# A fourth seven-product chunk in the late projection pairs, with two of the four weight sums of each group on GpSimd

## The chip, the cores and the metric

The kernel runs on one NeuronCore of a Trainium2 chip. The metric is the device time of one execution in microseconds (us); 2 us are about 0.2% of it. The engines are named as the profile names them: PE is the matrix engine, PEld its weight loads, DVE the vector engine, ACT the scalar engine, POOL is GpSimd, and SP issues most DMAs. Each engine works through its own instructions in a fixed order, and waits on semaphores for what others must deliver first.

## What is computed

One residual layer over 256 tokens of width 2048, in float32, followed by an RMSNorm. The layer projects the normalised input `h` to many column blocks, runs two token mixers, and merges their results:

```python
h = _rms_norm(x, norm_g)
proj = jnp.einsum('bsd,dn->bsn', h, w_in)          # q k v o za gates xb zb ga gb
ya = _mlstm_branch(q, k, v, o, za, gates, ...)     # 256 x 2048
yb = _rglru_branch(xb, zb, ...)                    # 256 x 2048
ya = jnp.einsum('bsw,wd->bsd', ya, w_branch_a)
yb = jnp.einsum('bsw,wd->bsd', yb, w_branch_b)
merged = sigmoid(ga) * ya + sigmoid(gb) * yb
out = _rms_norm(x + jnp.einsum('bsd,de->bse', merged, w_out), final_g)
```

The change touches the last projections: `w_branch_b`, the `gb` and `ga` blocks of `w_in`, `w_branch_a` and `w_out`. Each is a product of a 256 x 2048 activation with a 2048 x 2048 weight.

## The kernel before

**Numbers in two parts.** A float32 value is split into a rounded part `hi` (ACT copies it to the matmul type) and a rest `lo` (DVE subtracts `hi` from the value), and a product is made of three matmuls, hi·hi, hi·lo and lo·hi. So each weight chunk that arrives by DMA as `raw` (128 x 1024 float32, 512 KB) costs an ACT copy to `whi` and a DVE subtraction to `wlo` before PE can use it. There are six `raw` buffers and four each of `whi` and `wlo`.

**Pairs.** From line 163 on, `pair` computes two 512-column blocks at once. The inner dimension of 2048 is cut into eight chunks, `kq` = 0 to 7, of 256 rows each. A *plain* chunk (line 229) loads one `raw` for each of the two blocks and multiplies 2 blocks x 2 row halves x 2 token halves = 8 products of three matmuls each: 24 matmuls of 512 columns.

A chunk whose number is in `kqs` goes through `products` (line 186): the 2 x 2 blocks of weights and the 2 x 2 blocks of activations are combined by the Strassen-Winograd scheme, with seven products in place of eight, so 21 matmuls in place of 24. It needs sums of weight blocks, made as the weights arrive: `t1` (the tile tagged `vhi`) by the subtractions on lines 199 and 200, `t2` (`vlo`) by lines 203 and 204, each of the four on 128 x 512 elements. Line 203 reads the half of `t1` that line 200 made. Then `t1`, `t2` and the second `raw` are split into `whi` and `wlo` (lines 180 and 181: three tiles of 1024 columns) and half of the first `raw` into `b11` (512 columns). The same two `raw` tiles, 1 MB, are loaded as for a plain chunk. There is one `t1` and one `t2`, so the next group's `t1` is written only when the last reader of this one is done.

Four of the seven products gather in PSUM tiles `aux`, the others in `acc`. After the last such chunk of the pair, lines 252 to 256 combine the `aux` tiles into the destination (one ACT copy, four DVE additions that read PSUM), and line 262 adds `acc`.

The activations need sums too, once for each chunk number and activation: `make_form` (line 271) builds them with one addition, four sums on 128 x 128 and a split of 512 columns, all on DVE but one ACT copy.

**Which chunks.** The tables at the top say it. `S_WB`, `S_GB`, `S_GA` and `S_WA` list the chunk numbers of the two pairs of `w_branch_b`, `gb`, `ga` and `w_branch_a`: 0, 2 and 4 in each of these eight *late pairs*. `L_WB` to `L_WA` are the places in the order of the eight chunks at which they stand. The pair of `w_out` (`S_WO`, line 1034) has four such chunks already, as places 0, 2, 4 and 6. The order in time is: `w_branch_b` (two pairs), `gb` (two), `ga` (two), `w_branch_a` (two), one block of `w_out` without products (line 1021), the `w_out` pair, the last `w_out` block. Earlier pairs (`S_V`, `S_OZ`) are not touched.

**Order.** A scheduler orders each engine's instructions when the program is built. Weight loads, splits and sums are marked urgent (`urgent()`), so they stand in weight order, ahead of other work; the forms fill in between. After that the order of each engine is fixed.

POOL does little before: masks at the start, and small tensors of one column for the normalisation of the four heads (lines 860 and 861).

Of the kernel before, what the change touches and what calls it, by code (L numbers as in the profile page):

```python
# [10 lines left out]
F32R = mybir.dt.float32r  # L11
# [8 lines left out]
NB = 512  # L20
# [3 lines left out]
EPS = 1e-6  # L24
NEG = -1e30

S_WB, S_GB, S_GA, S_WA = [((0, 2, 4), (0, 2, 4))] * 4
S_OZ = (((4, 0), (2, 4)), ((4,), (1,)), ((4, 0), (2, 5)), ((4, 0), (0, 2)))
S_V = (((4,), (4,)), ((4,), (4,)))
S_WO = (0, 1, 2, 4)  # L30
L_WB, L_GB, L_GA, L_WA = ((0, 2, 4), (0, 2, 4)), ((0, 2, 4), (0, 2, 4)), ((0, 2, 4), (0, 2, 4)), ((0, 2, 4), (1, 3, 5))
L_WO = (0, 2, 4, 6)
H_FORMS = (4, 0)
PLAN = (dict(Y=('c0', '', '', 'c1',),
# [17 lines left out]
def hybrid_encoder(ctx: ExitStack, tc: tile.TileContext, x, xt, pk, bif, fg, wg, wi, wr, wa, wb, wo, out):  # L52
# [107 lines left out]
    def four(v):  # L160
        return v.rearrange("p (a b) -> p a b", b=S)

    def pair(src, xhi, xlo, forms, kqs, dst, b11, epilogue, sums=None, places=None, calm=False):
        aps = []
        accs = [acc_pair()[1] for _ in range(2)]
        banks = [[v[:, :NB], v[:, NB:]] for v in accs]
        began = set()
        places = places or kqs
        rest = [kq for kq in range(KT // KC) if kq not in kqs]
        seq = [kqs[places.index(i)] if i in places else rest.pop(0) for i in range(KT // KC)]  # L170
        kl = seq[-1]

        def mm(ps, a, b, wh, wl, stop):
            pe.matmul(ps, a, wh, start=id(ps) not in began, stop=False)  # L174
            began.add(id(ps))
            pe.matmul(ps, a, wl, start=False, stop=False)  # L176
            pe.matmul(ps, b, wh, start=False, stop=stop)  # L177

        def split(hi, lo, v):
            act.copy(hi, v)  # L180
            dve.tensor_sub(lo, v, f(hi))  # L181

        def wpair():
            return [wp.tile([P, KC * NB], F32R, tag=t, name=name(t), bufs=4) for t in ("whi", "wlo")]

        def products(kq, last):
            lf, rt_ = slice(0, NB), slice(NB, 2 * NB)
            with urgent():
                r1, r2 = [wp.tile([P, KC * NB], F32, tag="raw", name=name("raw"), bufs=6) for _ in range(2)]
                sp.dma_start(r1, src[0][kq])  # L190
                sp.dma_start(r2, src[1][kq])
                bh, bl = b11()
                split(bh, bl, r1[:, lf])
                if sums:
                    t1, t2 = sums()
                else:
                    t1, t2 = [four(hp.tile([P, 2 * NB], F32, tag=t, name=name("t"))) for t in ("vhi", "vlo")]
                v1, v2 = four(r1), four(r2)
                dve.tensor_sub(t1[:, :2], v1[:, 2:], v1[:, :2])
                dve.tensor_sub(t1[:, 2:], v2[:, :2], v1[:, 2:])  # L200
                h1, l1 = wpair()
                split(four(h1), four(l1), t1)
                dve.tensor_add(t2[:, :2], t1[:, 2:], v1[:, :2])
                dve.tensor_sub(t2[:, 2:], v2[:, 2:], t2[:, :2])
                h2, l2 = wpair()
                split(four(h2), four(l2), t2)
                h3, l3 = wpair()
                split(h3, l3, r2)
            fm = forms[kq]

            def xb(kk, tb):
                o = (kq * KC + kk) * S + tb * P
                return xhi(o, o + P), xlo(o, o + P)

            def sf(i):
                return [v[:, i * P:(i + 1) * P] for v in fm]

            if not aps:
                aps.extend(aux(i) for i in range(4))
            p1, p5, p7, p6 = aps  # L220
            mm(p1, *xb(0, 0), bh, bl, last)
            mm(p5, *sf(0), h1[:, lf], l1[:, lf], last)
            mm(p7, *sf(2), h1[:, rt_], l1[:, rt_], last)
            mm(p6, *sf(1), h2[:, lf], l2[:, lf], last)
            mm(banks[0][1], *xb(1, 1), h2[:, rt_], l2[:, rt_], False)
            mm(banks[0][0], *xb(1, 0), h3[:, rt_], l3[:, rt_], False)
            mm(banks[1][0], *sf(3), h3[:, lf], l3[:, lf], False)

        def plain(kq, jj):
            hi, lo = load_chunk(src[jj][kq])  # L230
            for kk in range(KC):
                o = (kq * KC + kk) * S
                c = slice(kk * NB, (kk + 1) * NB)
                for tb in range(2):
                    mm(banks[jj][tb], xhi(o + tb * P, o + tb * P + P), xlo(o + tb * P, o + tb * P + P),
                       hi[:, c], lo[:, c], kq == kl and kk == KC - 1)

        last = max(places)
        for i, kq in enumerate(seq[:last + 1]):
            if kq in kqs:  # L240
                products(kq, i == last)
            else:
                for jj in range(2):
                    if lanes or not aps:
                        tick()
                    plain(kq, jj)
        p1, p5, p7, p6 = aps
        if not dst:
            dst.extend(hp.tile([P, 2 * NB], F32, tag=t, name=name(t)) for t in ("to", "zz"))
        (d11, d21), (d12, d22) = [(v[:, :NB], v[:, NB:]) for v in dst]  # L250
        with urgent():
            act.copy(d11, p1)
            dve.tensor_add(d12, p6, d11)
            dve.tensor_add(d21, p7, d12)
            dve.tensor_add(d12, p5, d12)
            dve.tensor_add(d22, p5, d21)
        for jj in range(2):
            for kq in seq[last + 1:]:
                tick()
                plain(kq, jj)  # L260
            with urgent():
                dve.tensor_add(dst[jj], dst[jj], accs[jj])
                if not calm:
                    epilogue(jj)
            if calm:
                epilogue(jj)
# [632 lines left out]
    def h_form(kq, i):  # L899
        form("h", kq, i, parts=h_parts(kq))  # L900
# [9 lines left out]

    k_yb, k_h, k_ya = (sorted(set(sum(v, ()))) for v in (S_WB, S_GB + S_GA, S_WA))
    k_h = [kq for kq in k_h if kq not in hf]
    early = [lambda kq=kq, i=i: h_form(kq, i) for kq, i in zip(k_h, (3, 0, 1))]
    early += [lambda kq=kq, i=i: ya_form(kq, i) for kq, i in zip(k_ya[:1], (3, 0, 1)[len(early):])]

    for j in range(4):
        for i in range(2):
            both = half_tr(wi[BLK_ZB + j], i)
            if i == 0:
                zt = hp.tile([P, 2 * NB], F32, tag="zz" if j else "vhi", name=name("zt"))  # L920
                sg = hp.tile([P, 2 * NB], F32, tag="to" if j else "vlo", name=name("sg"))
            fold(zt[:, i * NB:(i + 1) * NB], both)
        act.activation(sg, zt, AF.Silu)
        dve.tensor_mul(sg, sg, hs[:, j * 1024:(j + 1) * 1024])
        ybh.append(sl(f"C{j}", F32R, 1024))
        ybl.append(sl(f"D{j}", F32R, 1024))
        act.copy(ybh[j], sg)
        dve.tensor_sub(ybl[j], sg, f(ybh[j]))
        if j == 0:
            fm_t.append(sl("PT", F32R))  # L930
        if j == 0:
            drain()
        for kq in (2 * j, 2 * j + 1):
            if kq in k_yb:
                form("b", kq, k_yb.index(kq), full=sg[:, (kq % 2) * NB:(kq % 2 + 1) * NB])
        if j == 1:
            early[0]()
    ybh, ybl = Cols(ybh, 1024), Cols(ybl, 1024)
    nb11 = [0]

# [5 lines left out]
    sgb = sl("E")  # L946
    sgv = [sgb[:, j * 1024:(j + 1) * 1024] for j in range(4)]
    for p in range(2):
        pair((wb[2 * p], wb[2 * p + 1]), ybh, ybl, forms("b"), S_WB[p], sgv[2 * p:2 * p + 2], b11, lambda jj: None, None, L_WB[p])
    for fn in early[1:]:  # L950
        fn()
    for p in range(2):
        gb = [sl(f"D{2 * p + i}", F32, 1024) for i in range(2)]

        def epi_gb(jj, p=p, gb=gb):
            act.activation(gb[jj], gb[jj], AF.Sigmoid)
            dve.tensor_mul(sgv[2 * p + jj], sgv[2 * p + jj], gb[jj])

        pair((wi[BLK_GB + 2 * p], wi[BLK_GB + 2 * p + 1]), hhi, hlo, forms("h"), S_GB[p], gb, b11, epi_gb, None, L_GB[p])
    ga = []  # L960
    for p in range(2):
        ga += [sl(f"C{2 * p + i}", F32, 1024) for i in range(2)]

        def epi_ga(jj, p=p):
            act.activation(ga[2 * p + jj], ga[2 * p + jj], AF.Sigmoid)

        pair((wi[BLK_GA + 2 * p], wi[BLK_GA + 2 * p + 1]), hhi, hlo, forms("h"), S_GA[p], ga[2 * p:], b11, epi_ga, None, L_GA[p])
    for i, kq in enumerate(k_ya[1:]):
        ya_form(kq, 1 + i)

    m_t = sl("HL", F32R, 8192)
    mh, ml = Cols([m_t[:, :4096]], 4096), Cols([m_t[:, 4096:]], 4096)
    for p in range(2):
# [17 lines left out]
                queue.extend([None] * (1 - p))  # L991
                queue.extend([lambda i=i, h=h: fin_m(i, h) for i in (2 * p, 2 * p + 1) for h in range(2)])

        pair((wa[2 * p], wa[2 * p + 1]), yah, yal, forms("a"), S_WA[p], wd, b11, epi_wa, None, L_WA[p], calm=True)

    y = sl("A")
    fgt = sl("PT")
# [33 lines left out]
        for tb in range(2):  # L1031
            out_piece(tb, jj * NB, (jj + 1) * NB, jj, dst[jj][:, tb * NB:(tb + 1) * NB])

    pair((wo[0], wo[1]), mh, ml, mf_, S_WO, dst, b11, epi_wo, None, L_WO)

    lw = sl("B", F32R)
    ch = []
# [92 lines left out]
```

## Time and profile before

| | before |
|---|---|
| median of 3 runs | 1014.27 us (1013.76 to 1014.4) |
| span of the profiled execution (its own time is not listed apart) | 1012.2 us |
| PE busy | 1003.0 us, 99% |
| DVE busy | 875.8 us, 87% |
| ACT busy | 628.6 us, 62% |
| POOL busy | 18.6 us, 2% |
| DMA moved | 199.32 MB, mean 197 GB/s |

The span runs from the first to the last instruction; the median is 2.1 us above it. Busy shares are means over stages that differ, so the stage of the late pairs, about 600 to 900 us, has to be read apart. The profile's duration of a matmul (0.39 us) includes the time in the array's pipeline, and the next one starts before it is over: how fast PE goes is read from starts.

### The profile page before, as it was taken

The numbers are of one execution on the slowest core, as the hardware profiler recorded it, in microseconds if no ns is written. First come the engines' busy times: TensorE is split into PE (matmuls) and PEld (weight loads), VectorE is DVE, ScalarE is ACT, GpSimd is POOL, SyncE is SP. The second block draws the span as 40 slices with busy tenths as digits, with TensorE's granted clock in tenths as the row PEclk, the third lists the DMA queues.
The fourth block names the chain that finished last, engine by engine and source line by source line (L and its number), as shares of the span: only waits on it lengthen the run. The fifth ranks groups of instructions, "written<-read, shape, count | busy, mean of one in ns | idle before, by whom it ended". The sixth has DMA issues, their size and how long they took to land.

```text
span 1012.2 us, 13718 instructions
## 1 busy us (share of the span) xinstructions
PE 1003.0 (99%) x5045; PEld 853.2 (84%) x5045; DVE 875.8 (87%) x1167; ACT 628.6 (62%) x825; POOL 18.6 (2%) x37
## 2 busy tenths in 40 slices
PE   9999999999999999999999999999999999999997
PEld 9888988888888888888888888888888888888886
DVE  6687898889769888997697888998898988999996
ACT  7546477756695786667955564655655656455562
POOL 1000000001001000000100000000000000000000
PEclk9999999999999999999999999999999999999999
DMA  9765446565555565657466466666566656568452
GB/s 349 263 208 157 160 153 198 173 213 197 167 190 167 177 197 184 210 167 227 146 199 208 155 208 188 212 212 201 187 216 200 219 177 212 184 217 336 161 200 83
DMA packets 56387, 199.32 MB, mean 197 GB/s; under 512 B 6400, under 2 KB 7424, under 8 KB 55936
## 3 DMA queue, kind: packets, MB, share of 16 engines
q1 hardware_dynamic: 55456, 197.13, 58.9%
q10 hardware_dynamic: 864, 1.32, 0.4%
q8 instruction: 39, 0.64, 0.3%
q14 instruction: 28, 0.23, 0.1%
HBM read 196.33 MB, written 2.10 MB: 196 GB/s over the span
## 4 chain that ended last, share of the span: by engine, by line
PE 97%; DVE 1%; DMA 1%; ACT 0%; issue 0%; ACTq 0%; SPq 0%; DVEq 0%
PE acc L176 17%; PE acc L177 17%; PE acc L174 17%; PE acc L315 16%; PE acc L318 8%; PE aux L176 3%; PE aux L174 3%; PE aux L177 3%; PE aux L855 1%; PE aux L721 1%; PE aux L720 1%; PE aux L719 1%; PE aux L1053 1%; PE aux L1052 1%; PE aux L1051 1%; PE acc L156 1%
## 5 line engine op out<-in xcount | busy, mean ns | idle before, releaser
L140 ACT CAST whi<-raw 128x1024 fp32r<-128x1024 f32 (+1 forms) x284 | 294.8, 1046 | 196.0 <-PE acc L177 99.7
L141 DVE TENSOR_TENSOR wlo<-raw,whi 128x1024 fp32r<-128x1024 f32 (+1 forms) x284 | 341.5, 1213 | 76.2 <-ACT whi L140 74.4
L176 PE MATMUL acc<-wlo,sHL 128*128 128x512 f32 x554 | 215.9, 390 | 0.0
L177 PE MATMUL acc<-whi,sHL 128*128 128x512 f32 x554 | 215.8, 390 | 0.0
L174 PE MATMUL acc<-whi,sHL 128*128 128x512 f32 x554 | 213.3, 390 | 0.0
L315 PE MATMUL acc<-sHL,whi 128*128 128x512 f32 x704 | 175.9, 393 | 0.0
L315 PEld LDWEIGHTS acc<-sHL,whi 128*128 128x128 f32 x704 | 127.4, 189 | 23.5
L174 PEld LDWEIGHTS acc<-whi,sHL 128*128 128x128 f32 x554 | 104.0, 188 | 21.2
L176 PEld LDWEIGHTS acc<-wlo,sHL 128*128 128x128 f32 x554 | 104.1, 188 | 21.0
L177 PEld LDWEIGHTS acc<-whi,sHL 128*128 128x128 f32 x554 | 104.0, 188 | 20.9
L318 PEld LDWEIGHTS acc<-sHL,wlo 128*128 128x128 f32 x704 | 95.3, 190 | 6.0
L180 ACT CAST whi<-t 128x1024 fp32r<-128x1024 f32 x70 | 73.5, 1051 | 42.9 <-PE acc L177 13.9
L318 PE MATMUL acc<-sHL,wlo 128*128 128x256 f32 x704 | 99.0, 283 | 0.0
L181 DVE TENSOR_TENSOR wlo<-t,whi 128x1024 fp32r<-128x1024 f32 x70 | 85.5, 1222 | 9.0 <-ACT whi L180 8.5
L180 ACT CAST whi<-raw 128x1024 fp32r<-128x1024 f32 x37 | 39.0, 1053 | 27.6 <-PE acc L177 16.9
L181 DVE TENSOR_TENSOR wlo<-raw,whi 128x1024 fp32r<-128x1024 f32 x37 | 45.2, 1222 | 8.7 <-ACT whi L180 8.7
L180 ACT CAST b<-raw 128x512 fp32r<-128x512 f32 x28 | 17.4, 621 | 39.2 <-DMA raw<-wi 16.5
L176 PE MATMUL acc<-wlo,sC 128*128 128x512 f32 x92 | 35.9, 390 | 0.4 <-DVE wlo L141 0.4
L176 PE MATMUL acc<-wlo,sA 128*128 128x512 f32 x92 | 36.0, 392 | 0.0
L177 PE MATMUL acc<-whi,sD 128*128 128x512 f32 x92 | 35.8, 389 | 0.0
L177 PE MATMUL acc<-whi,sB 128*128 128x512 f32 x92 | 35.8, 389 | 0.0
L174 PE MATMUL acc<-whi,sC 128*128 128x512 f32 x92 | 35.3, 389 | 0.0
(361 smaller groups left out, 1589.1 us busy)
## 6 DMA issues: line engine op xcount, KB each, us to landing
raw<-wi SPq DMA_DIRECT2D x254, 512.0 KB, 4.2
raw<-wb SPq DMA_DIRECT2D x32, 512.0 KB, 4.1
raw<-wa SPq DMA_DIRECT2D x32, 512.0 KB, 4.0
raw<-wo SPq DMA_DIRECT2D x32, 512.0 KB, 4.8
raw<-wr SPq DMA_DIRECT2D x8, 512.0 KB, 4.0
sB<-x SPq DMA_DIRECT2D x4, 512.0 KB, 7.7
sA<-x SPq DMA_DIRECT2D x1, 2048.0 KB, 7.9
sA<-xt SPq DMA_DIRECT2D x7, 256.0 KB, 6.7
```

The costliest lines, as they stand in the source:

```text
L140: last_copy[0] = act.copy(hi[:, r], raw[:, r]).ins
L141: last_sub[0] = dve.tensor_sub(lo[:, r], raw[:, r], f(hi[:, r])).ins
L156: pe.matmul(ps[tb], a, wl, start=False, stop=False)
L174: pe.matmul(ps, a, wh, start=id(ps) not in began, stop=False)
L176: pe.matmul(ps, a, wl, start=False, stop=False)
L177: pe.matmul(ps, b, wh, start=False, stop=stop)
L180: act.copy(hi, v)
L181: dve.tensor_sub(lo, v, f(hi))
L315: pe.matmul(ps[m], hi[:, o:o + P], hl_t[:, 2 * k * S:2 * (k + 1) * S], start=(k == 0), stop=(turn and k == KT - 1), skip_group_check=True)
L318: pe.matmul(ps[m][:, :S], lo[:, o:o + P], hhi(k * S, (k + 1) * S), start=False, stop=(not turn and k == KT - 1), skip_group_check=True)
L719: pe.matmul(dst, whi[:, o:o + P], xh[:, r], start=True, stop=False)
L720: pe.matmul(dst, whi[:, o:o + P], xl[:, r], start=False, stop=False)
```

## The change

All eight late pairs get a fourth chunk with seven products, number 6, and all have them at places 0, 2, 4 and 6. The two subtractions that make `t1` are issued on POOL wherever `pair` is given `t1_by=pool`: in the eight late pairs and in the `w_out` pair. Those are 9 pairs x 4 groups x 2 = 72 instructions on 128 x 512 elements. `t2` stays on DVE.

The forms follow: one more for each of `yb`, `h` and `ya`. The forms of `h` (chunks 2 and 6) are now made behind the `w_branch_b` pairs, two of `ya` behind the two `gb` pairs, and the last two behind the `ga` pairs, in the tiles `F0` and `F4` that held forms of `h`. The host lays out the weights of the added chunks for the scheme from the same tables.

```diff
-S_WB, S_GB, S_GA, S_WA = [((0, 2, 4), (0, 2, 4))] * 4
+S_WB, S_GB, S_GA, S_WA = [((0, 2, 4, 6), (0, 2, 4, 6))] * 4
-L_WB, L_GB, L_GA, L_WA = ((0, 2, 4), (0, 2, 4)), ((0, 2, 4), (0, 2, 4)), ((0, 2, 4), (0, 2, 4)), ((0, 2, 4), (1, 3, 5))
+L_WB, L_GB, L_GA, L_WA = [((0, 2, 4, 6), (0, 2, 4, 6))] * 4
...
-    def pair(src, xhi, xlo, forms, kqs, dst, b11, epilogue, sums=None, places=None, calm=False):
+    def pair(src, xhi, xlo, forms, kqs, dst, b11, epilogue, sums=None, places=None, calm=False, t1_by=None):
...
-                dve.tensor_sub(t1[:, :2], v1[:, 2:], v1[:, :2])
-                dve.tensor_sub(t1[:, 2:], v2[:, :2], v1[:, 2:])
+                for o, p_, q_ in ((t1[:, :2], v1[:, 2:], v1[:, :2]), (t1[:, 2:], v2[:, :2], v1[:, 2:])):
+                    (t1_by or dve).tensor_tensor(o, p_, q_, op=ALU.subtract)
...
-    early = [lambda kq=kq, i=i: h_form(kq, i) for kq, i in zip(k_h, (3, 0, 1))]
-    early += [lambda kq=kq, i=i: ya_form(kq, i) for kq, i in zip(k_ya[:1], (3, 0, 1)[len(early):])]
...
-        if j == 1:
-            early[0]()
...
-        pair((wb[2 * p], wb[2 * p + 1]), ybh, ybl, forms("b"), S_WB[p], sgv[2 * p:2 * p + 2], b11, lambda jj: None, None, L_WB[p])
-    for fn in early[1:]:
-        fn()
+        pair((wb[2 * p], wb[2 * p + 1]), ybh, ybl, forms("b"), S_WB[p], sgv[2 * p:2 * p + 2], b11, lambda jj: None, None, L_WB[p], t1_by=pool)
+    for i, kq in enumerate(k_h):
+        h_form(kq, i)
...
+        ya_form(k_ya[p], 2 + p)
...
-    for i, kq in enumerate(k_ya[1:]):
-        ya_form(kq, 1 + i)
+    for kq, slot_ in zip(k_ya[2:], H_FORMS[::-1]):
+        fslot["a", kq] = halves(sl(f"F{slot_}", F32R, 1024), 0)
+        make_form(fslot["a", kq], parts=[t(kq * NB, (kq + 1) * NB) for t in (yah, yal)])
...
-    pair((wo[0], wo[1]), mh, ml, mf_, S_WO, dst, b11, epi_wo, None, L_WO)
+    pair((wo[0], wo[1]), mh, ml, mf_, S_WO, dst, b11, epi_wo, None, L_WO, t1_by=pool)
```

Where the orders change, two places are shown. The first is DVE inside the second `gb` pair, from one group's `b11` on. Names with `t` are `t1` and `t2` (`t1` is written by lines 199 and 200), numbers tell buffers apart, and the brackets name whom the instruction waits for. Before:

```order
L181 TENSOR_TENSOR b11_1478_6740<-raw_1476_6736,b11_1478_6740 128x512 [waits DMAHW3_49,Activation_49]
L181 TENSOR_TENSOR wlo_1464_6672<-t_1460_6662,whi_1463_6671 128x1024 [waits Activation_49]
L199 TENSOR_TENSOR t_1479_6743<-raw_1476_6736 128x512 [waits DVE_49]
L200 TENSOR_TENSOR t_1479_6743<-raw_1477_6737,raw_1476_6736 128x512 [waits DMAHW4_49]
L181 TENSOR_TENSOR wlo_1466_6676<-raw_1457_6655,whi_1465_6675 128x1024 [waits Activation_49]
L203 TENSOR_TENSOR t_1480_6744<-t_1479_6743,raw_1476_6736 128x512 [waits DVE_49]
L141 TENSOR_TENSOR wlo_1470_6702<-raw_1468_6700,whi_1469_6701 128x1024 [waits DMAHW1_49,Activation_49]
L141 TENSOR_TENSOR wlo_1474_6720<-raw_1472_6718,whi_1473_6719 128x1024 [waits DMAHW2_49,Activation_49]
L204 TENSOR_TENSOR t_1480_6744<-raw_1477_6737,t_1480_6744 128x512 [waits DVE_49]
L181 TENSOR_TENSOR wlo_1482_6748<-t_1479_6743,whi_1481_6747 128x1024 [waits Activation_49]
```

And the same engine in the changed kernel, in the second `gb` pair, from the split that last reads one `t1` to the `b11` of the next group but one:

```order
L181 TENSOR_TENSOR wlo_1494_6791<-t_1491_6786,whi_1493_6790 128x1024 [waits Activation_49]
L204 TENSOR_TENSOR t_1492_6787<-raw_1489_6780,t_1492_6787 128x512 [waits DMAHW4_49,DVE_49]
L181 TENSOR_TENSOR b11_1510_6865<-raw_1508_6861,b11_1510_6865 128x512 [waits DMAHW7_49,Activation_49]
L181 TENSOR_TENSOR wlo_1496_6797<-t_1492_6787,whi_1495_6796 128x1024 [waits Activation_49]
L181 TENSOR_TENSOR wlo_1498_6801<-raw_1489_6780,whi_1497_6800 128x1024 [waits Activation_49]
L203 TENSOR_TENSOR t_1512_6869<-t_1511_6868,raw_1508_6861 128x512 [waits DVE_49,Pool_49]
L141 TENSOR_TENSOR wlo_1502_6827<-raw_1500_6825,whi_1501_6826 128x1024 [waits DMAHW5_49,Activation_49]
L204 TENSOR_TENSOR t_1512_6869<-raw_1509_6862,t_1512_6869 128x512 [waits DMAHW0_49,DVE_49]
L141 TENSOR_TENSOR wlo_1506_6845<-raw_1504_6843,whi_1505_6844 128x1024 [waits DMAHW6_49,Activation_49]
L181 TENSOR_TENSOR wlo_1514_6873<-t_1511_6868,whi_1513_6872 128x1024 [waits Activation_49]
L181 TENSOR_TENSOR wlo_1516_6879<-t_1512_6869,whi_1515_6878 128x1024 [waits Activation_49]
L181 TENSOR_TENSOR b11_1537_6969<-raw_1535_6965,b11_1537_6969 128x512 [waits DMAHW3_49,Activation_49]
```

The two rows that wrote `t1` are gone from DVE, and line 203 now waits for POOL. Four DVE rows stand between the split that last reads one `t1` (the first row) and line 203 of the next group (the sixth).

The second place is POOL in the same stretch. Before, it has no instruction there: its last ones are those of line 861 in the fourth head. Now it has two for each group, and nothing else:

```order
L200 TENSOR_TENSOR t_1471_6704<-raw_1468_6697 128x512 [waits DMAHW7_49,DVE_49]
L200 TENSOR_TENSOR t_1471_6704<-raw_1469_6698,raw_1468_6697 128x512 [waits DMAHW0_49]
L200 TENSOR_TENSOR t_1491_6786<-raw_1488_6779 128x512 [waits DMAHW3_49,DVE_49]
L200 TENSOR_TENSOR t_1491_6786<-raw_1489_6780,raw_1488_6779 128x512 [waits DMAHW4_49]
L200 TENSOR_TENSOR t_1511_6868<-raw_1508_6861 128x512 [waits DMAHW7_49,DVE_49]
L200 TENSOR_TENSOR t_1511_6868<-raw_1509_6862,raw_1508_6861 128x512 [waits DMAHW0_49]
```

The first of a group waits for its `raw` and for DVE, which has to have read the old `t1`; the second for the other `raw`. On ACT, the copy of `t1` into `whi` now waits for POOL instead of DVE, and the copies of the chunks behind it stand behind it in ACT's order.

More of the change, by code (lines that the diff above doesn't have):

```diff
@@ L957, in epi_gb @@
             dve.tensor_mul(sgv[2 * p + jj], sgv[2 * p + jj], gb[jj])
-        pair((wi[BLK_GB + 2 * p], wi[BLK_GB + 2 * p + 1]), hhi, hlo, forms("h"), S_GB[p], gb, b11, epi_gb, None, L_GB[p])
+        pair((wi[BLK_GB + 2 * p], wi[BLK_GB + 2 * p + 1]), hhi, hlo, forms("h"), S_GB[p], gb, b11, epi_gb, None, L_GB[p], t1_by=pool)
+        ya_form(k_ya[p], 2 + p)
     ga = []
@@ L965, in epi_ga @@
             act.activation(ga[2 * p + jj], ga[2 * p + jj], AF.Sigmoid)
-        pair((wi[BLK_GA + 2 * p], wi[BLK_GA + 2 * p + 1]), hhi, hlo, forms("h"), S_GA[p], ga[2 * p:], b11, epi_ga, None, L_GA[p])
-    for i, kq in enumerate(k_ya[1:]):
-        ya_form(kq, 1 + i)
+        pair((wi[BLK_GA + 2 * p], wi[BLK_GA + 2 * p + 1]), hhi, hlo, forms("h"), S_GA[p], ga[2 * p:], b11, epi_ga, None, L_GA[p], t1_by=pool)
+    for kq, slot_ in zip(k_ya[2:], H_FORMS[::-1]):
+        fslot["a", kq] = halves(sl(f"F{slot_}", F32R, 1024), 0)
+        make_form(fslot["a", kq], parts=[t(kq * NB, (kq + 1) * NB) for t in (yah, yal)])
     m_t = sl("HL", F32R, 8192)
@@ L992, in epi_wa @@
                 queue.extend([lambda i=i, h=h: fin_m(i, h) for i in (2 * p, 2 * p + 1) for h in range(2)])
-        pair((wa[2 * p], wa[2 * p + 1]), yah, yal, forms("a"), S_WA[p], wd, b11, epi_wa, None, L_WA[p], calm=True)
+        pair((wa[2 * p], wa[2 * p + 1]), yah, yal, forms("a"), S_WA[p], wd, b11, epi_wa, None, L_WA[p], calm=True, t1_by=pool)
     y = sl("A")
```

## The prediction

> **What bounds the kernel now.** I read the page first, then the windows of the late pairs, then starts in the timeline.
>
> ```profile
> span 1012.2 us, 13718 instructions
> PE 1003.0 (99%) x5045; PEld 853.2 (84%) x5045; DVE 875.8 (87%) x1167; ACT 628.6 (62%) x825; POOL 18.6 (2%) x37
> PE 97%; DVE 1%; DMA 1%; ACT 0%; issue 0%; ACTq 0%; SPq 0%; DVEq 0%
> ```
>
> The chain that ended last is 97% PE. A pipelined PE looks busy even where it is a little late, so its pace is read from starts. These two rows are the first and the last of 21 matmuls that follow one another in a `gb` pair:
>
> ```profile
> 693.21 0.39 PE L174 MATMUL acc<-whi,sHL 128*128 128x512 f32 x1
> ...
> 697.74 0.39 PE L177 MATMUL acc<-whi,sHL 128*128 128x512 f32 x1
> ```
>
> 20 steps in 4.53 us are 0.2265 us each. Before, a late pair has 3 x 21 + 5 x 24 = 183 matmuls: 41.45 us. The windows below run from one pair's line 253 to the next pair's (the last lies in the `w_out` pair); their columns are length, then busy time of PE, PEld, DVE, ACT and POOL, clock, DMA.
>
> ```profile
> 649.92:691.33 41.41, 41.41 (x184) 34.32 (x183) 36.69 (x42) 22.52 (x25) 0.00 (x0) 1.00 0.65 213
> 691.33:732.85 41.52, 41.52 (x185) 34.38 (x184) 37.98 (x43) 25.03 (x26) 0.00 (x0) 1.00 0.62 203
> 732.85:774.33 41.48, 41.48 (x184) 34.35 (x183) 38.05 (x43) 23.77 (x26) 0.00 (x0) 1.00 0.62 203
> 940.00:980.00 40.00, 40.00 (x184) 33.34 (x183) 37.15 (x50) 26.16 (x32) 0.00 (x0) 1.00 0.58 193
> ```
>
> 41.5 measured against 41.45 counted: PE sets the pace without gaps, at full clock. But DVE is busy 38.0 of 41.5 us, so the stage has a second limit 3.5 us behind the first. ACT and DMA (0.62) are far away.
>
> **What the change takes from PE.** Each added group saves three matmuls, 0.68 us; eight save 5.4 us. A pair is then 180 x 0.2265 = 40.8 us. The bytes loaded are the same, 1 MB for a chunk either way.
>
> **What it does to DVE.** Starts of successive rows give what an instruction occupies (durations overlap by some 0.08):
>
> ```profile
> 717.47 0.68 DVE L181 TENSOR_TENSOR b<-raw,b 128x512 fp32r<-128x512 f32 x1
> 718.16 1.23 DVE L181 TENSOR_TENSOR wlo<-t,whi 128x1024 fp32r<-128x1024 f32 x1
> 719.30 0.68 DVE L199 TENSOR_TENSOR t<-raw 128x512 f32<-128x512 f32 x1
> 719.90 0.69 DVE L200 TENSOR_TENSOR t<-raw,raw 128x512 f32<-128x512 f32 x1
> 720.50 1.22 DVE L181 TENSOR_TENSOR wlo<-raw,whi 128x1024 fp32r<-128x1024 f32 x1
> 721.64 0.69 DVE L203 TENSOR_TENSOR t<-t,raw 128x512 f32<-128x512 f32 x1
> 722.24 1.22 DVE L141 TENSOR_TENSOR wlo<-raw,whi 128x1024 fp32r<-128x1024 f32 x1
> ```
>
> 512 columns take 0.60 us, 1024 take 1.14. The rows that read PSUM cost the same:
>
> ```profile
> 710.59 1.21 DVE L262 TENSOR_TENSOR sD<-sD,acc 128x1024 f32<-128x1024 f32 x1
> 711.72 0.68 DVE L203 TENSOR_TENSOR t<-t,raw 128x512 f32<-128x512 f32 x1
> ...
> 732.85 0.69 DVE L253 TENSOR_TENSOR sD<-aux,sD 128x512 f32<-128x512 f32 x1
> 733.46 1.22 DVE L141 TENSOR_TENSOR wlo<-raw,whi 128x1024 fp32r<-128x1024 f32 x1
> ```
>
> A `gb` pair before: 19 splits and 4 rows of lines 262 and 957 at 1.14, 3 `b11`, 12 sums and 4 rows of lines 253 to 256 at 0.60: 37.6 us. After: 20 + 4 at 1.14, 4 `b11`, 8 sums and 4 rows at 0.60: 37.0 us. With all four sums left on DVE it would be 41.8, over PE's 40.8; so the fourth group hangs on what the two sums cost on POOL, and on what they cost DVE from there.
>
> **What the two sums cost on POOL.** The trace has no such instruction. Its nearest row reads one input of that size:
>
> ```profile
> 2.48 1.17 POOL L443 CAST st__166<-ident 128x512 fp32r<-128x512 f32 x2
> ...
> 240.19 0.55 POOL L861 TENSOR_TENSOR sq<-sq,mhalf 128x1 f32<-128x1 f32 x1
> ```
>
> Two casts in 1.17 us are 0.59 each. A sum reads twice as much: from 0.59 (the second input free) to 1.72 (twice the cast plus the 0.55 of a two-input instruction on one column). I take twice the cast, 1.17: 8 x 1.17 = 9.4 us a pair, little against 40.8 if POOL runs beside the others.
>
> (The Trainium skill, "GPSIMD Engine Reference", section "Performance versus the Vector engine", has 4497 ns for an addition of 2048 columns. A quarter is 1.12, an estimate from that page, and would make the sum below some 4 us smaller.)
>
> **Does POOL run beside DVE?** The small POOL instructions of the heads show it. Their wait is in their duration:
>
> ```profile
> 237.10 2.36 DVE L141 TENSOR_TENSOR wlo<-raw,whi 128x1024 fp32r<-128x1024 f32 x2
> 239.37 0.69 DVE L199 TENSOR_TENSOR t<-raw 128x512 f32<-128x512 f32 x1
> 240.78 0.75 DVE L862 SCALAR_TENSOR_TENSOR to<-aux,sq,zz 128x512 f32<-128x512 f32 x1 [0.72 <-POOL sq L861]
> ...
> 237.25 2.86 POOL L860 TENSOR_SCALAR sq<-sq 128x1 f32<-128x1 f32 x1 [200.26 <-ACT to L859]
> 240.83 0.19 POOL L860 TENSOR_SCALAR sq<-sq 128x1 f32<-128x1 f32 x1
> ```
>
> ```profile
> 427.84 1.22 DVE L141 TENSOR_TENSOR wlo<-raw,whi 128x1024 fp32r<-128x1024 f32 x1
> 428.98 0.69 DVE L200 TENSOR_TENSOR t<-raw,raw 128x512 f32<-128x512 f32 x1
> 429.58 1.22 DVE L141 TENSOR_TENSOR wlo<-raw,whi 128x1024 fp32r<-128x1024 f32 x1
> ...
> 428.80 2.05 POOL L860 TENSOR_SCALAR sq<-sq 128x1 f32<-128x1 f32 x1 [118.29 <-ACT to L859]
> ```
>
> Line 860 on one column takes 0.19 us beside line 862, which reads one operand from PSUM. The same instruction takes 2.86 and 2.05 beside DVE rows with both operands in SBUF, and ends at 240.11 and 430.85: within 0.06 of the end of the last DVE row (240.06 and 430.80). It did not get in between those rows. So POOL waits while DVE streams two SBUF operands, and nearly all DVE rows of a late pair do. What a long POOL read costs DVE no row shows: nothing, if it yields, or up to its whole 1.17 us, if it holds what DVE needs. I take the latter, since the hold in the rows is whole.
>
> The Trainium skill, "SBUF — State Buffer", section "Who interferes with whom", speaks against this change: a DVE instruction with two SBUF inputs and a GpSimd one that reads SBUF exclude each other, and the second fully blocks. The rows above agree for POOL (2.86 against 0.19); for DVE none here shows it. By that rule the sum is the one below; without it, that of the first rival.
>
> **The sum.** After the split that last reads `t1`, DVE has four rows (0.60 + 0.60 + 1.14 + 1.14 = 3.5 us) before line 203, which waits for POOL's next two sums. Alone, 2.3 us of POOL fit there. If DVE keeps POOL out, the sums start when DVE stands at line 203, and their 2.3 us are added to it. Behind line 203 the splits of the next plain chunk stand on DVE; behind the copy of `t1` into `whi`, the copies of `b11` and of the next chunks stand on ACT; PE waits for all of them, in its fixed order.
>
> So DVE and POOL in series need 37.0 + 9.4 = 46.4 us a pair. The rows that read PSUM (4 x 0.60 + 2 x 1.14 = 4.7 us) can hide one group's 2.3: 44.0. The eight pairs take 44.0 to 46.4 against 41.5: +20 to +39 us. Once DVE is the bound, its forms count too:
>
> ```profile
> 930.81 0.28 DVE L280 TENSOR_TENSOR xp<-xp 128x128 f32<-128x128 f32 x1
> 931.01 0.29 DVE L282 TENSOR_TENSOR xp<-xp 128x128 f32<-128x128 f32 x1
> ```
>
> A form is 0.60 + 4 x 0.20 + 0.60 = 2.0 us, and six instead of three lie among the pairs: +6. The `w_out` pair already has DVE nearly full (37.15 of 40 in the last window): it loses eight sums (-4.8) and gains 9.4 less 2.3 hidden: +2. DVE's lead when the first pair starts takes off some 3. Together +25 to +44; **I take the lower middle, +32: 1012.2 + 32 = 1044 of span, with the 2.1 us that the median lies above the span 1046 us.**
>
> **Rivals.**
> *POOL hides.* If DVE pays nothing for POOL's reads, or a sum costs it less than (40.8 - 37.0) / 8 = 0.48 us, PE stays the bound: 1014.3 - 5.4 = 1009 (1007 to 1011). For it: the 3.5 us of room, and that a long POOL read is not in the trace. Against it: 2.86 us for one column. From 0.48 us on, each further 0.1 costs 6 us over eight pairs.
> *POOL fits in.* It may find DVE's waits for ACT and the PSUM rows, so that only the DVE rows with two SBUF operands (37.0 - 4.7 = 32.3) add up with 9.4: 41.7 a pair, +2 over eight pairs, and up to 2 us a pair more for waits that don't match: 1014 to 1032. For it:
>
> ```profile
> 306.34 1.22 DVE L141 TENSOR_TENSOR wlo<-raw,whi 128x1024 fp32r<-128x1024 f32 x1
> 307.48 1.22 DVE L753 SCALAR_TENSOR_TENSOR sE<-sC,sE 128x1024 f32<-128x1024 f32 x1
> ...
> 307.23 0.38 POOL L860 TENSOR_SCALAR sq<-sq 128x1 f32<-128x1 f32 x1 [65.58 <-ACT to L859]
> ```
>
> Here POOL got in as DVE went from one kind of instruction to another (it ended at 307.61, line 753 started on time). Against it: in the rows further up it missed each change from TENSOR_TENSOR to TENSOR_TENSOR, and a late pair has little else on DVE.
> *The change does not do what it says.* The order shows the 72 sums on POOL and four groups a pair; no chance.
>
> **Chances.** Series, slower: 0.55. POOL fits in: 0.18, nearly half of it within 2 us of before. POOL hides: 0.27. Two microseconds, 0.2%, are about what a measurement tells from no change. So faster 0.27, same 0.10, slower 0.63. The forecast's own range is 1035 to 1058. The range from 1008 to 1058 takes in the rivals and leaves out the dearer sums (1.72 us each, 4.4 us more a pair, 1081).
>
> **What would show it.** If right: POOL's rows of line 200 are far longer than 1.2 us, or DVE stands idle before line 203 with POOL as releaser, some 2 us for each of 36 groups; PE has gaps with DVE as releaser; a pair's windows are 44 to 46 us. If POOL hides: 40.8 us a pair, and DVE rows unchanged at 0.60 and 1.14. DVE rows of 2 us would show the hold on DVE's side. I am wrong if DVE's rows keep their length and no row waits for POOL.

## The result, and the profile after

The changed kernel takes 1060.8 us (1059.75 to 1061.05, three runs) against 1014.27: slower by 4.6%, ratio 1.0462 with a 95% interval of 1.0446 to 1.0479. The forecast was slower, by 32 us; measured are 46.5, and 1060.8 lies just above the range of 1008 to 1058.

From the page of the changed kernel: the span, busy times, the chain that ended last, and four groups (busy time and mean length of one, then the idle time ahead of them and what ended most of it).

```profile
span 1058.8 us, 13872 instructions
PE 1017.8 (96%) x5021; PEld 851.3 (80%) x5021; DVE 896.7 (85%) x1160; ACT 642.2 (61%) x844; POOL 181.0 (17%) x109
PE 63%; DVE 15%; POOL 9%; issue 6%; DMA 5%; ACT 1%; POOLq 0%; DVEq 0%; ACTq 0%
...
L200 POOL TENSOR_TENSOR t<-raw 128x512 f32<-128x512 f32 x36 | 103.3, 2868 | 336.1 <-DVE wlo L181 200.5
L203 DVE TENSOR_TENSOR t<-t,raw 128x512 f32<-128x512 f32 x41 | 28.2, 688 | 39.9 <-POOL t L200 39.9
L200 POOL TENSOR_TENSOR t<-raw,raw 128x512 f32<-128x512 f32 x36 | 59.1, 1642 | 10.5 <-DMA raw<-wa 6.5
L181 DVE TENSOR_TENSOR b<-raw,b 128x512 fp32r<-128x512 f32 x36 | 35.7, 991 | 3.8 <-ACT b L180 3.7
```

The chain was 97% PE and is 63%: DVE, POOL and the steps between them have taken the rest. DVE stood 39.9 us ahead of line 203 for POOL, in 20 waits. The rows of `b11` have grown from 0.69 to 0.99 us on average, though they do the same work.

PE, which stood 2.3 us for others in the whole execution before, now stands some 34. Its largest waits (who waited for whom: us in total, times, longest):

```profile
PE acc L176 <- DVE wlo L141: 9.8, 10, 2.1
PE aux L174 <- ACT whi L180: 5.9, 3, 5.0
PE acc L157 <- DVE sHL L336: 4.9, 1, 4.9
PE acc L174 <- DVE sE L262: 3.7, 2, 1.9
```

Line 141 is the split of a plain chunk, line 180 the copies to the matmul type in a group; lines 262 and 336 stand at the end of a pair.

Two windows from one `gb` pair's line 253 to the next pair's, which answer to those of 41.5 us before (length, then busy PE, PEld, DVE, ACT, POOL):

```profile
719.33:765.56 46.23, 44.29 (x187) 33.98 (x185) 41.08 (x42) 26.24 (x29) 15.62 (x8) 1.00 0.55 183
765.56:809.81 44.25, 42.15 (x179) 32.95 (x179) 40.40 (x42) 25.02 (x27) 17.49 (x8) 1.00 0.55 190
```

And inside the first, two groups in order of time. DVE's timeline:

```profile
738.47 0.68 DVE L181 TENSOR_TENSOR b<-raw,b 128x512 fp32r<-128x512 f32 x1
739.07 1.22 DVE L181 TENSOR_TENSOR wlo<-raw,whi 128x1024 fp32r<-128x1024 f32 x1
740.21 1.22 DVE L141 TENSOR_TENSOR wlo<-raw,whi 128x1024 fp32r<-128x1024 f32 x1
743.86 0.69 DVE L203 TENSOR_TENSOR t<-t,raw 128x512 f32<-128x512 f32 x1 [2.43 <-POOL t L200]
...
747.34 1.78 DVE L181 TENSOR_TENSOR b<-raw,b 128x512 fp32r<-128x512 f32 x1
749.05 2.32 DVE L181 TENSOR_TENSOR wlo<-t,whi 128x1024 fp32r<-128x1024 f32 x1
```

POOL's timeline over the same stretch:

```profile
737.50 5.07 POOL L200 TENSOR_TENSOR t<-raw 128x512 f32<-128x512 f32 x1 [11.53 <-DVE wlo L181]
742.54 1.29 POOL L200 TENSOR_TENSOR t<-raw,raw 128x512 f32<-128x512 f32 x1
746.90 1.68 POOL L200 TENSOR_TENSOR t<-raw 128x512 f32<-128x512 f32 x1 [3.08 <-DVE wlo L181]
748.54 1.74 POOL L200 TENSOR_TENSOR t<-raw,raw 128x512 f32<-128x512 f32 x1
```

Both directions are here. The POOL sum at 737.50 gets nowhere while DVE rows follow one another; DVE is through at 741.43, and the sum ends at 742.57, 1.14 later. The second, with DVE idle, takes 1.29, and only then does line 203 go on: 2.43 us lost. In the next group POOL starts in a gap of DVE, and the `b11` row of 0.68 takes 1.78: it ends 0.54 after the POOL sum does (748.58). The split behind it takes 2.32 in place of 1.22, again past the end of a POOL sum (750.28). Of the 36 first sums of a group, 13 took from 3.9 to 7.3 us like the one at 737.50; the other 23 took 1.3 to 2.4.

Lengths of the stretches, from the end of a pair's second row of line 262 to the next pair's, in us (wb is `w_branch_b`, wa `w_branch_a`; the last column holds the `w_out` block and the `w_out` pair). The end of the first wb pair stands as a time in the span.

| kernel | first wb ends at | wb 2 | gb 1 | gb 2 | ga 1 | ga 2 | wa 1 | wa 2 | w_out |
|---|---|---|---|---|---|---|---|---|---|
| before | 629.8 | 40.6 | 41.4 | 41.1 | 41.2 | 41.5 | 42.7 | 42.1 | 69.5 |
| changed | 634.7 | 51.8 | 44.7 | 44.9 | 44.3 | 44.0 | 44.1 | 48.7 | 78.9 |
| all sums on DVE | 635.4 | 47.6 | 43.4 | 46.0 | 45.0 | 43.4 | 41.0 | 43.0 | 75.5 |
| POOL only fills | 628.4 | 44.4 | 41.5 | 41.3 | 40.8 | 40.8 | 40.8 | 42.2 | 74.3 |
| three groups, last at place 6 | 630.8 | 41.6 | 41.7 | 43.1 | 41.4 | 41.5 | 41.5 | 42.9 | 73.0 |
| three groups, `t1` on POOL | 628.4 | 44.5 | 42.7 | 43.2 | 41.8 | 41.6 | 41.6 | 43.8 | 73.7 |
| groups at 0, 2, 3, 4, POOL sums | 634.9 | 51.6 | 46.2 | 47.7 | 44.2 | 46.2 | 44.3 | 46.2 | 74.7 |

The loss is not even: the second wb pair (+11.2), the last wa pair (+6.6) and the `w_out` stretch (+9.4) hold 27 of the 46.6 us by which the spans differ. In the last wa pair much of it comes from one POOL sum. POOL's timeline there, and PE's:

```profile
914.88 7.32 POOL L200 TENSOR_TENSOR t<-raw 128x512 f32<-128x512 f32 x1 [11.54 <-DVE wlo L181]
```

```profile
924.55 1.22 PE L174 MATMUL aux<-whi,sF 128*128 128x512 f32 x2 [4.98 <-ACT whi L180]
```

The sum is held for 7.32 us, ACT's copy of `t1` waits 4.38 us for POOL, and PE waits 4.98 us for that copy.

### The profile page after: what moved, and what is told of

It reads as the page before. It is cut to its first block, busy times and chain, and to the rows that moved or that the text cites. A ratio compares the mean times of both kernels' runs of the same rounds, so it can differ in the third digit from the quotient of the medians.

```text
span 1058.8 us, 13872 instructions
## 1 busy us (share of the span) xinstructions
PE 1017.8 (96%) x5021; PEld 851.3 (80%) x5021; DVE 896.7 (85%) x1160; ACT 642.2 (61%) x844; POOL 181.0 (17%) x109
## 4 chain that ended last, share of the span: by engine, by line
PE 63%; DVE 15%; POOL 9%; issue 6%; DMA 5%; ACT 1%; POOLq 0%; DVEq 0%; ACTq 0%
PE acc L315 15%; PE acc L176 9%; PE acc L177 9%; PE acc L174 9%; POOL t L200 9%; PE acc L318 8%; DVE wlo L181 4%; DVE wlo L141 4%; DMA raw<-wi 3%; PE aux L174 1%; DMA raw<-wa 1%; DVE b L181 1%; PE aux L177 1%; PE aux L176 1%; PE aux L855 1%
## 5 line engine op out<-in xcount | busy, mean ns | idle before, releaser
L140 ACT CAST whi<-raw 128x1024 fp32r<-128x1024 f32 (+1 forms) x268 | 277.6, 1044 | 192.0 <-PE acc L177 90.7
L141 DVE TENSOR_TENSOR wlo<-raw,whi 128x1024 fp32r<-128x1024 f32 (+1 forms) x268 | 323.1, 1214 | 69.2 <-ACT whi L140 67.6
L177 PE MATMUL acc<-whi,sHL 128*128 128x512 f32 x530 | 207.6, 392 | 0.0
L174 PE MATMUL acc<-whi,sHL 128*128 128x512 f32 x530 | 205.0, 393 | 1.8 <-DVE sE L262 1.8
L200 POOL TENSOR_TENSOR t<-raw 128x512 f32<-128x512 f32 x36 | 103.3, 2868 | 336.1 <-DVE wlo L181 200.5
L180 ACT CAST whi<-t 128x1024 fp32r<-128x1024 f32 x86 | 90.1, 1051 | 64.1 <-DVE t L204 21.4
L181 DVE TENSOR_TENSOR wlo<-t,whi 128x1024 fp32r<-128x1024 f32 x86 | 111.0, 1298 | 11.4 <-ACT whi L180 10.9
L203 DVE TENSOR_TENSOR t<-t,raw 128x512 f32<-128x512 f32 x41 | 28.2, 688 | 39.9 <-POOL t L200 39.9
L200 POOL TENSOR_TENSOR t<-raw,raw 128x512 f32<-128x512 f32 x36 | 59.1, 1642 | 10.5 <-DMA raw<-wa 6.5
L181 DVE TENSOR_TENSOR wlo<-raw,whi 128x1024 fp32r<-128x1024 f32 x45 | 57.1, 1269 | 2.7 <-ACT whi L180 2.6
L181 DVE TENSOR_TENSOR b<-raw,b 128x512 fp32r<-128x512 f32 x36 | 35.7, 991 | 3.8 <-ACT b L180 3.7
```

Source lines behind the costliest of these rows:

```text
L140: last_copy[0] = act.copy(hi[:, r], raw[:, r]).ins
L141: last_sub[0] = dve.tensor_sub(lo[:, r], raw[:, r], f(hi[:, r])).ins
L200: (t1_by or dve).tensor_tensor(o, p_, q_, op=ALU.subtract)
```

## The experiments

The theory was that a POOL sum and a DVE row with both operands in SBUF shut each other out. The rivals were plain latency (line 203 waits for a slow engine, nothing more), and the ends of the pairs (the last group at place 6 leaves lines 252 to 262 one plain chunk to hide behind). The kernel before was timed beside them at 1013.3 to 1013.4 us.

| experiment | us | ratio to before, 95% interval |
|---|---|---|
| four groups, all sums on DVE | 1045.3 | 1.0314 (1.0296 to 1.0331) |
| three groups, `t1` on POOL | 1026.4 | 1.0126 (1.0111 to 1.0141) |
| changed, POOL only fills | 1021.4 | 1.0079 (1.0062 to 1.0096) |
| before, POOL sums that nobody reads | 1049.0 | 1.0348 (1.0332 to 1.0363) |
| changed, groups at 0, 2, 3, 4 | 1060.2 | 1.0458 (1.0442 to 1.0474) |
| the same, all sums on DVE | 1034.6 | 1.0207 (1.0193 to 1.0221) |
| before, last group at place 6 | 1023.6 | 1.0102 (1.0088 to 1.0116) |
| before, four groups in ga alone | 1016.6 | 1.0035 (1.0022 to 1.0047) |
| changed, forms of h and ya left out | 1051.8 | 1.0376 (1.0356 to 1.0396) |
| changed, last wa pair early | 1056.7 | 1.0430 (1.0409 to 1.0450) |
| fills, no forms, last wa pair early | 1013.1 | 0.9998 (0.9988 to 1.0008) |

### Fills in place of sums

```diff
-                    (t1_by or dve).tensor_tensor(o, p_, q_, op=ALU.subtract)
+                    if t1_by:
+                        for _ in range(2):
+                            pool.memset(o, 0.0)
+                    else:
+                        dve.tensor_tensor(o, p_, q_, op=ALU.subtract)
```

> The changed kernel with each POOL subtraction replaced by two POOL fills of the same 128 x 512 half of t1, so t1 is zero and the sums that the products need are left out. POOL still works some 2.2 us for each group at the same place, and line 203 still waits for it, but POOL reads nothing. Exclusion theory, where it is the reading that shuts out: fills keep 0.55 us each, no DVE row is longer than 1.25 us, PE is the bound again: 1007 to 1014 us. Latency theory (the loss is that line 203 waits for a POOL that takes over 2 us, with no exclusion): POOL takes nearly as long, so most of the loss stays, 1040 us or more.

1021.4 us: 39 us under the changed kernel, though POOL is still in the loop. Groups of instructions of this kernel between 600 and 1000 us:

```profile
L202 POOL MEMSET t<- 128x512 f32 x132 | 63.9, 528 | 311.2 <-DVE wlo L181 311.2
...
L181 DVE TENSOR_TENSOR wlo<-t,whi 128x1024 fp32r<-128x1024 f32 x68 | 82.4, 1220 | 5.3 <-ACT whi L180 5.1
...
L181 DVE TENSOR_TENSOR b<-raw,b 128x512 fp32r<-128x512 f32 x34 | 23.3, 686 | 4.3 <-ACT b L180 4.3
```

POOL's fills run beside DVE at 0.53 us each, some 1.9 us a group where two undisturbed sums take 2.6, and no DVE row is longer than before. So it is POOL's reading that excludes, and latency is not the cause: the row of line 203 waits 0.6 us for POOL in all. The time is still over the 1007 to 1014 that I gave. What stays, +8 against before where -5.4 was to be expected, is hardly POOL's: PE's longest waits here are 3.4 us for the split of line 336 and 2.8 us for the second wb pair's line 262. The Trainium skill, "SBUF — State Buffer", section "Who interferes with whom", says the same: a GpSimd instruction that only writes does not contend with a DVE instruction of two SBUF inputs. The 686 and 528 ns agree.

### All sums on DVE

```diff
-        pair(..., L_WB[p], t1_by=pool)
+        pair(..., L_WB[p])
```

(and so in all five calls)

> The changed kernel with the subtractions for t1 back on DVE: four groups in every late pair, nothing on POOL. Exclusion theory (a POOL sum of 1.29 us and a DVE row with two SBUF operands shut each other out, so each sum lengthens DVE's line by up to its whole length): DVE needs 39.5 us in a w_branch_b or ga pair, 41.8 in a gb pair and some 44 in a w_branch_a pair against PE's 40.8, so the time is 1010 to 1022 us, 40 us or more under the changed kernel. Tail theory (the loss comes from the fourth chunk: its last group ends one chunk before the pair does, so lines 253 to 262 hold PE up): most of the loss stays, 1040 us or more.

1045.3 us, 15.5 under the changed kernel. That is far over the 1010 to 1022 of the exclusion theory, and inside the range of the tail theory. One window of the second gb pair:

```profile
726.40:772.30 45.90, 41.84 (x181) 33.39 (x180) 43.79 (x51) 26.19 (x28) 0.00 (x0) 1.00 0.60 205
```

DVE is busy 43.8 us, that is 41.8 of the pair and a form of 2.0: with the fourth group it is the bound, as counted. By the upper end of my count (1022) that accounts for at most 9 of the 32 us. PE's largest waits in this kernel point to the ends of the pairs for more of it:

```profile
PE acc L174 <- DVE sE L262: 6.5, 2, 3.3
PE acc L157 <- DVE sHL L336: 3.5, 2, 2.6
```

So exclusion is not the whole loss. Still, the two sums on POOL, which were to relieve DVE, cost 15 us more than they saved. An account from the trace of the changed kernel: 72 x 0.60 = 43 us leave DVE. Back come 39.9 us ahead of line 203 and some 20 us in longer rows (36 `b11` rows at 0.99 for 0.69, 86 and 45 splits at 1.30 and 1.27 for 1.22). That is 60 for 43, 17 net, near the 15 measured.

### POOL with three groups, and POOL for nobody

The first is the kernel before with `t1_by=pool`. The second leaves all sums on DVE and adds the same two once more:

```diff
+                if extra:
+                    t0 = hp.tile([P, NB], F32, tag="scr", name=name("scr"), bufs=1).rearrange("p (a b) -> p a b", b=S)
+                    pool.tensor_tensor(t0, v1[:, 2:], v1[:, :2], op=ALU.subtract)
+                    pool.tensor_tensor(t0, v2[:, :2], v1[:, 2:], op=ALU.subtract)
```

> The kernel before, three groups in a late pair, with t1 on POOL in the late pairs and the w_out pair (56 sums). Exclusion theory: DVE 34.0 + 6 x 1.29 = 41.7 us in a gb pair, with waits that don't match, against PE's 41.5: 1 to 3 us a pair and 5 to 9 us in the w_out pair, 1025 to 1045 us; POOL rows of line 200 are stretched to several us here too. Tail theory: no fourth chunk, so the time of before, 1012 to 1017 us.

> The kernel before with all sums on DVE as they are, and POOL making the two subtractions of each late group and w_out group once more (56 sums) into a tile that nobody reads. Nobody waits for POOL except the next load into the raw tile that it read. Exclusion theory: DVE 37.6 + 6 x 1.29 = 45.3 us a pair where POOL gets in, less where it is starved and runs in DVE's idle time: 1018 to 1050 us, with DVE rows of up to 2.4 us. Latency theory: nothing waits for the result, so the time of before, 1012 to 1017 us.

1026.4 and 1049.0 us, both as exclusion says. In the second, nobody waits for the sums, and yet it costs 35.6 us, for 56 sums. Three groups of DVE rows between 590 and 1050 us:

```profile
L141 DVE TENSOR_TENSOR wlo<-raw,whi 128x1024 fp32r<-128x1024 f32 x99 | 123.4, 1264 | 7.6 <-ACT whi L140 7.6
...
L181 DVE TENSOR_TENSOR b<-raw,b 128x512 fp32r<-128x512 f32 x28 | 33.0, 1180 | 10.1 <-ACT b L180 10.1
L199 DVE TENSOR_TENSOR t<-raw 128x512 f32<-128x512 f32 x26 | 25.4, 976 | 0.8 <-DMA raw<-wa 0.8
```

1.18 and 0.98 for 0.69: DVE is held. Part of the cost is a late load, since a `raw` tile is free only when POOL has read it: in the `w_out` pair a load waited 9.4 us for a stretched POOL sum, the loads of the next group stood behind it, and PE stood 7.8 us for the copy of `b11`. How much of the 35.6 is of this kind was not separated.

### The ends of the pairs

```diff
-L_WB, L_GB, L_GA, L_WA = ((0, 2, 4), (0, 2, 4)), ((0, 2, 4), (0, 2, 4)), ((0, 2, 4), (0, 2, 4)), ((0, 2, 4), (1, 3, 5))
+L_WB, L_GB, L_GA, L_WA = [((0, 2, 6), (0, 2, 6))] * 4
```

> The kernel before, three groups and all sums on DVE, with the last group of each late pair at place 6 (places 0, 2 and 6). No work is added and nothing is on POOL. Tail theory: the ends alone cost time, 1018 to 1030 us. If place 6 is harmless: 1012 to 1016 us.

1023.6 us: 10.4 lost with no more work and no POOL. The largest part, 3.5 of the 8.7 us by which the two profiled spans differ, is in the `w_out` stretch (73.0 for 69.5), where PE stands 3.06 us for line 336, the split of the merged activation behind the last wa pair. Before, it had no wait there. This kernel's timeline (start, duration, instruction, then the wait ahead of it):

```profile
938.32 0.50 PE L157 MATMUL acc<-whi,sHL 128*128 128x512 f32 x1 [3.06 <-DVE sHL L336]
```

In the timeline of the changed kernel the same matmul waits 4.93:

```profile
973.07 0.79 PE L157 MATMUL acc<-whi,sHL 128*128 128x512 f32 x1 [4.93 <-DVE sHL L336]
```

With the last wa pair alone early, in the changed kernel:

```diff
-L_WB, L_GB, L_GA, L_WA = [((0, 2, 4, 6), (0, 2, 4, 6))] * 4
+L_WB, L_GB, L_GA = [((0, 2, 4, 6), (0, 2, 4, 6))] * 3
+L_WA = (0, 2, 4, 6), (0, 2, 3, 4)
```

> The changed kernel with the groups of the last w_branch_a pair alone at places 0, 2, 3 and 4. Tail theory: PE's 4.9 us wait for line 336 at the start of the w_out block goes, and with it the slow clock behind it: 1053 to 1058 us. If that wait has another cause: 1060 us or more.

1056.7 us (1054.4 to 1058.9), 4.1 less, and the `w_out` stretch falls from 78.9 to 74.8. The wait for line 336 is gone.

All late pairs early, with POOL sums and with DVE sums:

> The changed kernel with the four groups of every late pair at places 0, 2, 3 and 4 instead of 0, 2, 4 and 6, so three plain chunks follow the last group and not one; POOL still makes t1. Tail theory (beside the exclusion, PE stands at the ends of pairs because lines 252 to 262 have only one plain chunk to hide behind): the losses at the ends of the w_branch_b and w_branch_a pairs go, 1035 to 1050 us against 1061. If the ends cost nothing: 1058 us or more, since the work is the same.

> The same places 0, 2, 3 and 4 with all sums on DVE (the kernel of 1045 us otherwise). Tail theory: 1018 to 1034 us, near what DVE's own work says (39.5 to 44 us a pair and some forms). If the 32 us of that kernel are DVE's throughput alone: 1042 us or more.

With DVE sums 1034.6, 10.7 less than at 0, 2, 4 and 6: the ends again, though not quite down to the 1034 I gave. With POOL sums 1060.2, nothing gained: a miss. The `w_out` stretch does fall (74.7), but the gb pairs grow to 46.2 and 47.7 and the second ga pair to 46.2. The largest of PE's waits in that kernel:

```profile
PE aux L174 <- ACT whi L180: 19.3, 17, 3.5
```

17 times PE stood for a copy on line 180, inside a group. Groups that follow one another leave 21 x 0.2265 = 4.8 us from one `t1` to the next. DVE's own rows of a group, three splits of 1.14 and three rows of 0.60, are 5.2, and POOL's two sums 2.6 more. So what the ends gave was paid between the groups.

### The forms

```diff
-        h_form(kq, i)
+        fslot["h", kq] = hf[H_FORMS[i]]
```

(and so for the four forms of ya)

> The changed kernel with the six forms of h and ya that lie among the pairs not computed (old tiles stand in for them, so those sums are left out). Series theory (DVE's rows and POOL's sums add up, so whatever DVE does in a pair is on the path): about 2.0 us for each form, 8 to 14 us less than the changed kernel, most of it in the second w_branch_b pair, where four of them lie. If forms fill DVE's waits: within 2 us of the changed kernel.

1051.8 us, 9 less. The second wb pair falls by 7.9 us, from 51.8 to 43.9, near four forms at 2.0. The window of that pair in the changed kernel, with DVE's busy time as the third engine:

```profile
634.70:686.50 51.80, 44.98 (x180) 34.23 (x179) 46.92 (x62) 25.99 (x29) 21.22 (x8) 0.93 0.52 174
```

And the same pair without the forms:

```profile
631.30:675.20 43.90, 41.92 (x181) 33.45 (x180) 37.80 (x40) 23.61 (x26) 15.63 (x8) 1.00 0.56 192
```

46.9 of DVE and then 37.8. Where DVE and POOL are in series, each DVE instruction is on the path. The granted clock (the number ahead of the DMA share) rises from 0.93 to 1.00 between the two windows, so a part of the 7.9 is PE's pace; it was not separated.

### All three taken away, and a fourth group where there is room

> POOL fills in place of its sums, the six forms not computed, and the last w_branch_a pair at places 0, 2, 3 and 4: t1 and the forms are left out of the computation. If exclusion, forms and that end are all that took the saving of 5.4 us away: 1007 to 1011 us, under the kernel before. If the fourth chunk costs something else: 1014 us or more.

1013.1 us, the same as before, and between my 1011 and 1014. Without exclusion, forms and the late end the loss is gone, but of PE's saving of 5.4 only about 1 us appears in the span. Four of the seven stretches between the first wb pair and `w_out` are at PE's 40.8 to 41.0; what holds the others at 41.5 to 43.5 stays open.

> Four groups in the two ga pairs alone, at places 0, 2, 4 and 5, all sums on DVE; three elsewhere, places as before. DVE needs 39.5 us there against PE's 40.8, so two groups save 1.4 us if nothing else moves: 1011 to 1014 us. The forms of h and ya that move can take that back: up to 1018 us.

1016.6 us, 3.4 lost. The first ga pair takes 41.8, the second gb pair 39.9, but the second wb pair 43.0, where the forms of `h` now lie (60 DVE instructions in its stretch, 54 before), and the second ga pair 43.1. No kernel here beats the one before.

## Why the prediction was wrong, and where it was right

- **PE paces the late pairs at 0.2265 us a matmul, with DVE 3.5 us behind.** Right: with fills, three pairs in a row take 40.8 us, as 180 matmuls should.
- **A POOL sum takes 1.17 us.** Nearly: 1.26 to 1.29 undisturbed. The estimate from the Trainium skill's figure ("GPSIMD Engine Reference", section "Performance versus the Vector engine") was 1.12.
- **POOL waits while DVE streams two SBUF operands, and holds DVE in turn.** Right in both directions, the second of which no row had shown: 5.07 us for a sum of 1.29, and 2.32 for a split of 1.22.
- **The sums start when DVE stands at line 203, and add to it.** Right for 20 of the 36 groups: 39.9 us in 20 waits of 2.0 on average. In most of the others POOL got in earlier, and what it cost shows as longer DVE rows, some 20 us.
- **A pair in series takes 44.0 to 46.4 us.** Right at the low end for gb 1 to wa 1: 44.0 to 44.9. There is some luck in the match: with all sums on DVE the stretches gb 1 to ga 2 take 43.4 to 46.0, so the length alone does not show the series; the waits at line 203 and the fills (40.8 to 41.5 there) do. The second wb pair (+11.2, with four forms in it) and the last wa pair (+6.6) are far over the 4.9 that a pair was to lose at most. Together with the two wb pairs and the last wa pair, the eight lost 37 us; the forecast of 32, less 2 for `w_out`, had 30.
- **Six forms instead of three, +6.** The price holds as DVE's work (2.0 each), but four of them fall in one pair.
- **The `w_out` pair, +2.** This is the step that failed: +9.4 measured for the `w_out` stretch. With +2 there the time would have been 1053, inside the range. Two things were mis-sized. First, the +2 was a change of DVE's work, not of time: by the prediction's own figures 37.15 + 2.3 = 39.5 us of DVE would still have fitted into the 40. The kernel with three groups and POOL sums, its last wa pair at the old places, shows +4.2 in that stretch. Second, I left out what the last group's move, from place 5 to place 6 of the last wa pair, does to the chain behind it: PE stood 4.9 us for line 336 at the start of the `w_out` block, and moving that one pair's groups forward gives back 4.1. The two make 8.3 of the 9.4.
- **DVE's lead takes off some 3.** No run shows this term: the first wb pair ended 4.9 us later than before. Without the forms it ended 3.4 earlier than in the changed kernel.
- **The ends were not in the sum at all.** I gave the places no price, as if only the number of groups counted; they cost 10.4 us with three groups and no POOL. The terms overlap (an early place gained nothing beside POOL sums in the other pairs), so they don't add up to 46.6 exactly.
- **The clock was not in the sum either.** The prediction took PE's pace as 0.2265 us throughout. The last section shows half that pace behind long waits; over the whole execution this can be at most some 10 us.
- **POOL fits in, 0.18.** It gave 41.7 us a pair; 44.0 is the least measured. POOL did often get in early, but DVE's rows grew for it.
- **All four sums on DVE would be 41.8 against 40.8.** Right as DVE's work (43.8 with a form), and still no guide to the time: that kernel lost 32 us.
- **POOL hides, 0.27.** It needed POOL not to read, and even with fills the time was 1021.4 and not 1009.

## What to carry to other kernels

Before moving work from a full DVE to POOL, look in the trace for a small POOL instruction beside DVE rows that read two SBUF operands; if its duration swells to the end of those rows, expect the move to add POOL's time to DVE's in place of running beside it. POOL work that only writes is another matter. And when more work is put late in a stage, price what must drain after the last piece, with the work left to cover it: here late places alone cost 10 us.

## What the runs showed that was not expected

PE's waits had an echo. After the last group of the second wb pair PE stood twice for some 2 us with three matmuls between, and then ran at half pace for 4 us more. Two windows of the changed kernel there, whose columns end with the granted clock, DMA and GB/s:

```profile
680.00:685.00 5.00, 1.70 (x5) 0.62 (x3) 5.00 (x7) 1.04 (x1) 0.00 (x0) 0.77 0.50 138
685.00:690.00 5.00, 4.52 (x12) 3.59 (x13) 5.00 (x8) 1.57 (x2) 0.00 (x0) 0.55 0.57 193
```

And PE's timeline in them and just behind:

```profile
682.66 0.62 PE L176 MATMUL aux<-wlo,sF 128*128 128x512 f32 x1
683.08 0.63 PE L177 MATMUL aux<-whi,sF 128*128 128x512 f32 x1
...
686.04 0.63 PE L176 MATMUL acc<-wlo,sHL 128*128 128x512 f32 x1
686.47 0.63 PE L177 MATMUL acc<-whi,sHL 128*128 128x512 f32 x1
...
690.87 0.39 PE L174 MATMUL acc<-whi,sHL 128*128 128x512 f32 x1
691.10 0.40 PE L176 MATMUL acc<-wlo,sHL 128*128 128x512 f32 x1
```

Starts are 0.42 to 0.43 us apart, from 682.66 on, and then 0.23 again. Some nine matmuls at the slow pace behind the second wait cost about 2 us on top of the waits. The runs agree on when this happens: in the kernels whose longest single wait of PE is 1.6 us or less (before, three groups with `t1` on POOL, groups at 0, 2, 3, 4 with DVE sums, four in ga alone, all three taken away) the mean granted clock is 0.998 or 0.999; in the others, with a wait of 3.1 us or more, it is 0.986 to 0.997. That long waits cause the slow pace is read from this and from the order in time; no run tested it alone.

In the changed kernel the mean is 0.988, and the clock is low in, or just behind, the stretches where the loss is large: 0.94 from 634 to 686 us, 0.96 from 686 to 730, 0.93 from 908 to 957 and 0.98 from 957 to 1036, against 1.00 in between. The difference of 0.010 from before is some 10 us of 1058.8, an upper bound for its share of the loss, since PE also stood still in part of that time.

The Trainium skill, "TensorE: Matmul & The Clock Gate", section "Part 1: The HAM clock gate (the "warmup" mystery)", describes such a gate: after a window of about 3.4 us that was idle, the array's clock is halved. The 0.43 against 0.23 agrees.
